# Seven-product blocks of a feed-forward: earlier loads, one sum moved from a DMA to GpSimd, stream sums moved forward

## The chip, the cores and the metric

The kernel runs on one core of a Trainium2 chip. The metric is the device time of one execution in microseconds (us). The engines are named as the profile names them: PE is TensorE's matmul, PEld its weight load, DVE is VectorE, ACT is ScalarE, POOL is GpSimd, SP is SyncE, which here only issues DMAs.

## What is computed

The reference is a two-layer trunk over 256 latent tokens and 256 context tokens of width 1024. Each layer does a SwiGLU feed-forward half-step, a mixer with three head groups, and a second feed-forward half-step; both streams use the same weights. The change touches one of the four feed-forwards, the first of layer 1:

```python
def swiglu(h, w1, w2):
    g, u = jnp.split(h @ w1, 2, axis=-1)
    return (jax.nn.silu(g) * u) @ w2
x   = x   + 0.5 * gate_x * swiglu(ada_rms(x,   ...), w1, w2)
ctx = ctx + 0.5 * gate_c * swiglu(ada_rms(ctx, ...), w1, w2)
```

Width 2816 is handled as 22 column blocks of 128, in two halves of 11 (`JH`).

## The kernel before, in words

Every operand is held as a high part (float32r) and a low part (the rest), so that a product is three matmuls: high by high, high by low, low by high. ACT makes the high part of a weight tile (a cast), DVE the low part (a subtraction of two SBUF tiles). The tokens lie along the free dimension: columns 0 to 255 are the latent stream, 256 to 511 the context.

In three of the feed-forwards a column block is computed directly: gate and up weights by both streams at once. In layer 1's first feed-forward the first four blocks of the first half are direct (`DIRECT = 4`); the first two of these take the latent stream's products first and the context's after them, since the context's norm is later. The other 7 blocks of the first half and all 11 of the second are seven-product blocks (class `Seven`): the 2x2 block product of (gate, up halves) by (latent, context) is done with seven products of half size instead of eight. This needs sums of weights and sums of the streams:

- `sums` (line 463) makes four sums of the two streams in two rounds `q` of 12 steps, on DVE, with ACT casting each result to `th` and DVE writing the rest to `tl`. The steps are put in the list `bg` ahead of the direct blocks 2 and 3 (line 671); `pump`, called after each product, takes one step for each 512 columns of product.
- `load(j)` (line 493) lets SP load the gate block into a `wr` buffer (three of these) and the up block's first half twice into `cb[:, j % 2]`, and POOL add two more halves to it by DMAs with an accumulating write (lines 502 and 503). This gives `q`.
- `load_u(j)` loads the up block's second half into `ur` (one buffer).
- `second(j)` (line 530) adds `q`'s first half to the first half of `wr`, by an accumulating DMA from POOL. It overwrites what `low("g", j)` reads. `fourth(j)` (line 534, L537) adds the two halves of `wr` on DVE. The result is `r`.
- `high` and `low` make the parts of `g`, `q`, `r` and `u`. The parts `wh` and `wl` have four buffers each.

`go` (line 559) issues a block's seven products of 12 matmuls each on PE, in the order g, q, g, q, r, r, u, and the combinations of their results on DVE and ACT (L583 to L593). After each product it calls `nxt(slot)`, which places the preparation of the next block between: `high("g")` at slot 0, `low("g")` and `second` at 1, `high("q")` and `load_u` at 2, `low("q")` and the load of the block after next at 3, `fourth` and `high("r")` at 5, `low("r")` at 6, where the high part of the gated result (`aTh`) has just been made. Each engine and each DMA queue works its instructions in the order in which they are issued here, and waits by semaphores alone. The first seven-product block of a half is prepared by the list `prepare(j)`: in the last direct block for the first half, beside the last `down` products for the second.

Of the kernel before, what the change touches and what calls it, by code (L numbers as in the profile page):

```python
# [20 lines left out]
KT = D // 128  # L21
# [111 lines left out]
def tile_hybrid_dit(ctx: ExitStack, tc: tile.TileContext, t_x, t_c, t_cb, t_ada0, t_ada, t_adab, t_nw, t_w1, t_w2,  # L133
# [42 lines left out]
    def flush_due():  # L176
        while due:
            due.pop(0)[1]()
# [38 lines left out]
    with tc.manual_schedule():  # L217
# [230 lines left out]
        class Seven:  # L448
# [14 lines left out]
            def sums(self, q):  # L463
# [13 lines left out]

                def parts(i, n, sign=1.0):
                    h, lo = self.th[:, i, k0], self.tl[:, i, k0]
                    S.activation(out=h, in_=x[n], func=AF.Copy, scale=sign)  # L480
                    V.scalar_tensor_tensor(out=lo, in0=x[n], scalar=sign, in1=h.bitcast(F32), op0=ALU.mult,
                                           op1=ALU.subtract)

                def comb(n, p, r, op):
                    V.tensor_tensor(out=x[n], in0=x[p], in1=x[r], op=op)

                return [lambda: (work(), whole(0, k0, b)), lambda: whole(1, k0, a),
                        lambda: comb(1, 1, 0, ALU.subtract), lambda: parts(0, 1),
                        lambda: whole(2, k1, b), lambda: comb(0, 2, 0, ALU.subtract), lambda: parts(2, 0),
                        lambda: comb(2, 2, 1, ALU.add), lambda: parts(1, 2, -1.0),  # L490
                        lambda: whole(0, k1, a), lambda: comb(0, 2, 0, ALU.subtract), lambda: parts(3, 0)]

            def load(self, j):
                if j >= 2 * JH:
                    return
                g, u = t_w1[self.l, self.f, j, 0], t_w1[self.l, self.f, j, 1]
                r = wpool.tile([128, CHUNK], F32, tag="wr", name="wr", bufs=RAW_BUFS)
                SP.dma_start(out=r, in_=g)
                q = cb[:, j % 2]
                for k in range(2):  # L500
                    SP.dma_start(out=q[:, 512 * k:512 * k + 512], in_=u[:, 0:512])
                G.dma_start(out=q[:, 0:512], in_=u[:, 512:1024], accum_op=ALU.add)
                G.dma_start(out=q[:, 512:1024], in_=g[:, 0:512], accum_op=ALU.add)
                self.raw["g", j] = self.raw["r", j] = r
                self.raw["q", j] = q

# [23 lines left out]
            def second(self, j):  # L530

                G.dma_start(out=self.raw["r", j][:, 0:512], in_=self.raw["q", j][:, 0:512], accum_op=ALU.add)

# [5 lines left out]
            def prepare(self, j):  # L539

                return [lambda: self.high("g", j), lambda: (self.low("g", j), self.second(j)),
                        lambda: self.high("q", j), lambda: self.low("q", j), lambda: self.fourth(j),
                        lambda: self.high("r", j), lambda: self.low("r", j)]

# [54 lines left out]
        def ffn(l, f, lead, norms, steps=None, tail=None):  # L599
# [7 lines left out]
            with tc.tile_pool(name="ffn", bufs=1) as fp:  # L607
# [5 lines left out]
                for half in range(2):  # L613
# [34 lines left out]
                    if half == 0 and not one:  # L648
# [5 lines left out]
                        for c, kt in LEAD[lead]:  # L654
                            if c == len(w):
                                w.append(ws.take(0))
                            up(w[c], ps[c], a, b, kt)
                        flush_due()
                        for j in range(2):
                            for a, b in first[1:]:  # L660
# [6 lines left out]
                    if seven and half == 0:  # L667
                        first_j = seven.prepare(j1)
                        seven.load(j1)
                        seven.load(j1 + 1)  # L670
                        bg.extend([s for q in range(2) for s in seven.sums(q)] + [lambda: seven.load_u(j1)])
                        pace[0], pace[1] = SUMS, 0.0
                    for j in range(j0, j1):
# [13 lines left out]
                    for j in range(j1, JH if seven else j1):  # L687
                        n = half * JH + j

                        def nxt(slot):  # L690
# [12 lines left out]
                            elif slot == 0:  # L703
                                seven.high("g", n + 1)
                            elif slot == 1:
                                seven.low("g", n + 1)
                                seven.second(n + 1)
                            elif slot == 2:
                                seven.high("q", n + 1)
                            elif slot == 3:  # L710
                                seven.low("q", n + 1)
                                if j < JH - 2:
                                    seven.load(n + 2)
                            elif slot == 5:
                                seven.fourth(n + 1)
                                seven.high("r", n + 1)
                            elif slot == 6:
                                seven.low("r", n + 1)

# [9 lines left out]
                    for m in range(KT - 2 if split_tail else KT):  # L729
                        a, b = 0, T * len(streams)  # L730
                        wa, wb = ws.take(), ws.take(AHEAD - 1)
                        ps = mm_bank("d")
                        if seven and half == 0:
                            if m == KT - 3:
                                seven.load(JH)
                                seven.load(JH + 1)
                            if m >= KT - 2:
                                for s in seven.prepare(JH)[0 if m == KT - 2 else 4:4 if m == KT - 2 else 8]:
                                    s()
                        down(m, wa, wb, a, b, ps)  # L740
                        residual(l, i, m, ps, 0, streams)
                        if half == 1:
# [1036 lines left out]
```

## Time and profile before

| | |
|---|---|
| time, median of 3 runs | 1876.81 us (1873.68 to 1882.07) |
| the profiled execution | 1881.24 us, its span 1879.5 us |
| PE busy | 1815.5 us, 97% of the span |
| PEld, DVE, ACT, POOL busy | 82%, 65%, 37%, 9% |
| mean DMA traffic | 150 GB/s |

The span is the time from the first to the last instruction; the execution's own time has 1.7 us more around it. A busy share is an average over stages with different limits, so the rows below are taken from the stage that the change touches, 1060 to 1420 us. The granted clock (PEclk) is 1.00 at TensorE's level of 2.4 GHz and 0.50 at 1.2 GHz.

### The profile page before, as it was taken

The page shows a single profiled execution, that of the slowest core. Times are in us where ns is not written, and L with a number is a line of the kernel's source. Part 1 is how long each engine was busy: PE and PEld are TensorE (multiplying, and loading weights), DVE is VectorE, ACT ScalarE, POOL GpSimd, SP SyncE. Part 2 cuts the span into 40 slices and gives each one's busy share as a digit, 9 for nine tenths or more (in the row PEclk, how much of TensorE's full clock was granted, in tenths as well). Part 3 has the DMA queues.
Part 4 walks back from the last instruction along what each step waited for, and adds up shares of the span by engine and source line. Part 5 has one row for each costly group of instructions (what it writes and reads, how often), then busy time and mean ns, then how long its engine had stood idle before and what let it go on. Part 6 is the DMA issues. An engine that isn't in the chain of part 4 may idle for free. (4 is left out here: it accounts for less than half of the span.)

```text
span 1879.5 us, 27717 instructions
## 1 busy us (share of the span) xinstructions
PE 1815.5 (97%) x10944; PEld 1542.7 (82%) x10944; DVE 1213.8 (65%) x2064; ACT 690.9 (37%) x1131; POOL 174.9 (9%) x207
## 2 busy tenths in 40 slices
PE   7999999999999999999999988898889999999999
PEld 5788888887669888888888878888887877889999
DVE  5788778665455658777777576735664645666665
ACT  3332222245542333222222334423433455354443
POOL 0000000002133300000000001101210113410000
PEclk9999999999999999999999999999999999999999
DMA  7755656333121226555576335645763342335655
GB/s 292 261 177 193 201 181 200 113 110 118 56 63 45 68 68 222 182 171 199 184 264 230 97 99 136 163 121 122 176 162 101 100 130 68 112 117 169 191 176 157
DMA packets 96835, 281.72 MB, mean 150 GB/s; under 512 B 11329, under 2 KB 18113, under 8 KB 96577
## 3 DMA queue, kind: packets, MB, share of 16 engines
q1 hardware_dynamic: 88928, 265.79, 43.2%
q0 software_dynamic: 7776, 14.16, 4.8%
q8 instruction: 86, 1.41, 0.3%
q14 instruction: 45, 0.36, 0.1%
HBM read 274.14 MB, written 1.05 MB: 146 GB/s over the span
## 5 line engine op out<-in xcount | busy, mean ns | idle before, releaser
L98 DVE TENSOR_TENSOR wl<-wr,wh 128x1024 fp32r<-128x1024 f32 (+1 forms) x340 | 364.3, 1100 | 107.2 <-ACT wh L87 105.8
L87 ACT CAST wh<-wr 128x1024 fp32r<-128x1024 f32 (+1 forms) x340 | 312.2, 945 | 187.9 <-PE d L205 124.6
L204 PE MATMUL d<-aTh,wh 128*128 128x512 f32 (+1 forms) x770 | 268.9, 349 | 0.0
L205 PE MATMUL d<-aTl,wh 128*128 128x512 f32 (+1 forms) x770 | 268.4, 349 | 0.0
L206 PE MATMUL d<-aTh,wl 128*128 128x512 f32 (+1 forms) x770 | 268.4, 349 | 0.0
L204 PE MATMUL g<-hTh,wh 128*128 128x512 f32 (+2 forms) x592 | 208.6, 352 | 1.5 <-ACT wh L87 0.5
L205 PE MATMUL g<-hTl,wh 128*128 128x512 f32 (+2 forms) x592 | 208.3, 352 | 1.3 <-DVE hTl L354 1.1
L206 PE MATMUL g<-hTh,wl 128*128 128x512 f32 (+2 forms) x592 | 207.5, 351 | 0.6 <-DVE wl L98 0.5
L206 PE MATMUL u<-hTh,wl 128*128 128x512 f32 (+2 forms) x592 | 207.4, 350 | 0.4 <-DVE wl L98 0.4
L204 PE MATMUL u<-hTh,wh 128*128 128x512 f32 (+2 forms) x592 | 207.0, 350 | 0.0
L205 PE MATMUL u<-hTl,wh 128*128 128x512 f32 (+2 forms) x592 | 206.9, 350 | 0.0
L204 PEld LDWEIGHTS d<-aTh,wh 128*128 128x128 f32 x770 | 144.5, 188 | 21.3
L205 PEld LDWEIGHTS d<-aTl,wh 128*128 128x128 f32 x770 | 144.5, 188 | 21.2
L206 PEld LDWEIGHTS d<-aTh,wl 128*128 128x128 f32 x770 | 144.5, 188 | 21.2
L278 DVE CUSTOM_DVE_ANT_0 aw<-aw,cb 128x1024 f32<-128x1024 f32 x128 | 155.0, 1223 | 2.4
L212 PE MATMUL nat<-wh,hTh 128*128 128x512 f32 (+2 forms) x384 | 137.1, 357 | 0.0
L637 ACT CAST aTh<-sg 128x512 fp32r<-128x512 f32 x66 | 40.9, 619 | 256.0 <-DVE sg L633 242.3
L429 DVE SCALAR_TENSOR_TENSOR xT<-d,mod,xT 128x256 f32<-128x256 f32 x112 | 50.3, 480 | 126.6 <-PE d L206 126.6
L214 PE MATMUL nat<-wh,hTl 128*128 128x512 f32 (+2 forms) x384 | 128.0, 333 | 0.4 <-DVE hTl L354 0.4
L213 PE MATMUL nat<-wl,hTh 128*128 128x512 f32 (+2 forms) x384 | 127.7, 333 | 0.0
L204 PEld LDWEIGHTS g<-hTh,wh 128*128 128x128 f32 x592 | 111.6, 189 | 19.0 <-ACT hTh L371 1.5
L205 PEld LDWEIGHTS g<-hTl,wh 128*128 128x128 f32 x592 | 111.9, 189 | 17.9 <-DVE hTl L354 2.3
(261 smaller groups left out, 3432.2 us busy)
## 6 DMA issues: line engine op xcount, KB each, us to landing
wr<-in_w_dram SPq DMA_DIRECT2D x158, 512.0 KB, 4.3
aw<-in_ada_dram SPq DMA_DIRECT2D x144, 512.0 KB, 5.4
wr<-in_wi_dram SPq DMA_DIRECT2D x56, 512.0 KB, 3.6
wr<-in_w_dram SPq DMA_DIRECT2D x64, 384.0 KB, 3.7
wr<-in_w_dram SPq DMA_DIRECT2D x64, 320.0 KB, 2.9
cb<-in_w_dram SPq DMA_DIRECT2D x36, 256.0 KB, 5.8
cb<-in_w_dram POOLq DMA_DIRECT2D x36, 256.0 KB, 4.5
wr<-in_wo_dram SPq DMA_DIRECT2D x16, 512.0 KB, 3.6
```

The source lines that it names most:

```text
L87: self.nc.scalar.copy(out=h[:, :n], in_=self.raw[i][:, :n])
L98: self.nc.vector.tensor_tensor(out=lo[:, :n], in0=t[:, :n], in1=h[:, :n].bitcast(F32), op=ALU.subtract)
L204: PE.matmul(out=ps, lhsT=wh[:, col:col + 128], rhs=hh[rhs_sl], start=start, stop=False)
L205: PE.matmul(out=ps, lhsT=wh[:, col:col + 128], rhs=hl[rhs_sl], start=False, stop=False)
L206: PE.matmul(out=ps, lhsT=wl[:, col:col + 128], rhs=hh[rhs_sl], start=False, stop=stop)
L212: PE.matmul(out=ps, lhsT=hh[lhs_sl], rhs=wh[:, wc], start=start, stop=False)
L213: PE.matmul(out=ps, lhsT=hh[lhs_sl], rhs=wl[:, wc], start=False, stop=False)
L214: PE.matmul(out=ps, lhsT=hl[lhs_sl], rhs=wh[:, wc], start=False, stop=stop)
L278: V.tensor_tensor_reduce(out=junk, in0=t, in1=cb[:, s], scale=1.0, scalar=0.0, op0=ALU.mult, op1=ALU.add, accum_out=mod[l][:, 8 * r + b, s ...
L429: V.scalar_tensor_tensor(out=xT[:, m, s * T:s * T + T], in0=ps[:, s * T - c0:s * T - c0 + T], scalar=mod[l][:, 24 * i + 16 + m, s:s + 1], ...
L637: S.copy(out=aTh[:, j], in_=sg)
```

## The change

- `sums` issues the same work in another order: a cast follows directly on its sum, and the subtraction behind it stands one sum later. Its first step asks that the norms of both streams have been issued.
- These steps, and `load_u(DIRECT)`, go in the list ahead of the context's products of the first two direct blocks, at the same pace of one step for 512 columns. The adding DMAs of the first two seven-product blocks follow in the list.
- `load` is split: SP's loads stay in `load`, POOL's two adding DMAs are `add`. In a block, `load` of the block after next moves from slot 3 to slot 0 and `add` to slot 4.
- `second` is an addition on POOL instead of an accumulating DMA.
- `high("g")` moves from slot 0 of a block to slot 6 of the block before it, `low("g")` and `second` from slot 1 to slot 0. `prepare` ends with the `high("g")` of the block after it.
- In the last `down` products of the first half the preparation is issued behind the products of its `m` instead of in front of them.

```diff
--- before.py
+++ after.py
@@ -475,20 +475,27 @@
                 def whole(n, k, c):
                     V.tensor_tensor(out=x[n], in0=hTh[:, k, c].bitcast(F32), in1=hTl[:, k, c].bitcast(F32), op=ALU.add)
 
-                def parts(i, n, sign=1.0):
-                    h, lo = self.th[:, i, k0], self.tl[:, i, k0]
-                    S.activation(out=h, in_=x[n], func=AF.Copy, scale=sign)
-                    V.scalar_tensor_tensor(out=lo, in0=x[n], scalar=sign, in1=h.bitcast(F32), op0=ALU.mult,
-                                           op1=ALU.subtract)
+                def high(i, n, sign=1.0):
+                    S.activation(out=self.th[:, i, k0], in_=x[n], func=AF.Copy, scale=sign)
+
+                def low(i, n, sign=1.0):
+                    V.scalar_tensor_tensor(out=self.tl[:, i, k0], in0=x[n], scalar=sign,
+                                           in1=self.th[:, i, k0].bitcast(F32), op0=ALU.mult, op1=ALU.subtract)
 
                 def comb(n, p, r, op):
                     V.tensor_tensor(out=x[n], in0=x[p], in1=x[r], op=op)
 
-                return [lambda: (work(), whole(0, k0, b)), lambda: whole(1, k0, a),
-                        lambda: comb(1, 1, 0, ALU.subtract), lambda: parts(0, 1),
-                        lambda: whole(2, k1, b), lambda: comb(0, 2, 0, ALU.subtract), lambda: parts(2, 0),
-                        lambda: comb(2, 2, 1, ALU.add), lambda: parts(1, 2, -1.0),
-                        lambda: whole(0, k1, a), lambda: comb(0, 2, 0, ALU.subtract), lambda: parts(3, 0)]
+                def normed(f):
+                    f.when = lambda: all(kt in feeds[self.l, 2 * self.f, n].done for kt in range(KT) for n in range(2))
+                    return f
+
+                sub = ALU.subtract
+                return [normed(lambda: (work(), whole(0, k0, b))), lambda: whole(1, k0, a),
+                        lambda: (comb(1, 1, 0, sub), high(0, 1)), lambda: whole(2, k1, b),
+                        lambda: low(0, 1), lambda: (comb(0, 2, 0, sub), high(2, 0)),
+                        lambda: (comb(2, 2, 1, ALU.add), high(1, 2, -1.0)), lambda: low(2, 0),
+                        lambda: whole(0, k1, a), lambda: low(1, 2, -1.0),
+                        lambda: (comb(0, 2, 0, sub), high(3, 0)), lambda: low(3, 0)]
 
             def load(self, j):
                 if j >= 2 * JH:
@@ -499,10 +506,16 @@
                 q = cb[:, j % 2]
                 for k in range(2):
                     SP.dma_start(out=q[:, 512 * k:512 * k + 512], in_=u[:, 0:512])
+                self.raw["g", j] = self.raw["r", j] = r
+                self.raw["q", j] = q
+
+            def add(self, j):
+
+                if j >= 2 * JH:
+                    return
+                g, u, q = t_w1[self.l, self.f, j, 0], t_w1[self.l, self.f, j, 1], self.raw["q", j]
                 G.dma_start(out=q[:, 0:512], in_=u[:, 512:1024], accum_op=ALU.add)
                 G.dma_start(out=q[:, 512:1024], in_=g[:, 0:512], accum_op=ALU.add)
-                self.raw["g", j] = self.raw["r", j] = r
-                self.raw["q", j] = q
 
             def load_u(self, j):
                 if j >= 2 * JH:
@@ -529,7 +542,8 @@
 
             def second(self, j):
 
-                G.dma_start(out=self.raw["r", j][:, 0:512], in_=self.raw["q", j][:, 0:512], accum_op=ALU.add)
+                r = self.raw["r", j]
+                G.tensor_tensor(out=r[:, 0:512], in0=r[:, 0:512], in1=self.raw["q", j][:, 0:512], op=ALU.add)
 
             def fourth(self, j):
 
@@ -539,8 +553,9 @@
             def prepare(self, j):
 
                 return [lambda: self.high("g", j), lambda: (self.low("g", j), self.second(j)),
-                        lambda: self.high("q", j), lambda: self.low("q", j), lambda: self.fourth(j),
-                        lambda: self.high("r", j), lambda: self.low("r", j)]
+                        lambda: self.high("q", j), lambda: self.low("q", j),
+                        lambda: (self.fourth(j), self.high("r", j)), lambda: self.high("g", j + 1),
+                        lambda: self.low("r", j)]
 
             def product(self, ps, w, j, k, t):
                 wh, wl = self.part[w, j]
@@ -656,6 +671,10 @@
                                 w.append(ws.take(0))
                             up(w[c], ps[c], a, b, kt)
                         flush_due()
+                        if seven:
+                            bg.extend([s for q in range(2) for s in seven.sums(q)])
+                            bg.append(lambda: seven.load_u(DIRECT))
+                            pace[0], pace[1] = SUMS, 0.0
                         for j in range(2):
                             for a, b in first[1:]:
                                 for kt in range(KT):
@@ -665,11 +684,10 @@
                             ws.prefetch(j + 2)
                     j1 = DIRECT * (1 - half) if seven else JH
                     if seven and half == 0:
-                        first_j = seven.prepare(j1)
                         seven.load(j1)
                         seven.load(j1 + 1)
-                        bg.extend([s for q in range(2) for s in seven.sums(q)] + [lambda: seven.load_u(j1)])
-                        pace[0], pace[1] = SUMS, 0.0
+                        bg.extend([lambda: seven.add(j1), lambda: seven.add(j1 + 1)])
+                        first_j = seven.prepare(j1)
                     for j in range(j0, j1):
                         if seven and j == j1 - 1:
                             bg.extend(first_j)
@@ -701,20 +719,22 @@
                                 elif slot in (1, 3, 5):
                                     ws.prefetch((slot + 1) // 2)
                             elif slot == 0:
-                                seven.high("g", n + 1)
-                            elif slot == 1:
                                 seven.low("g", n + 1)
                                 seven.second(n + 1)
+                                if j < JH - 2:
+                                    seven.load(n + 2)
                             elif slot == 2:
                                 seven.high("q", n + 1)
                             elif slot == 3:
                                 seven.low("q", n + 1)
-                                if j < JH - 2:
-                                    seven.load(n + 2)
+                            elif slot == 4 and j < JH - 2:
+                                seven.add(n + 2)
                             elif slot == 5:
                                 seven.fourth(n + 1)
                                 seven.high("r", n + 1)
                             elif slot == 6:
+                                if j < JH - 2:
+                                    seven.high("g", n + 2)
                                 seven.low("r", n + 1)
 
                         seven.go(n, lambda sg, between: gated(j, sg, between), nxt)
@@ -730,14 +750,15 @@
                         a, b = 0, T * len(streams)
                         wa, wb = ws.take(), ws.take(AHEAD - 1)
                         ps = mm_bank("d")
-                        if seven and half == 0:
-                            if m == KT - 3:
-                                seven.load(JH)
-                                seven.load(JH + 1)
-                            if m >= KT - 2:
-                                for s in seven.prepare(JH)[0 if m == KT - 2 else 4:4 if m == KT - 2 else 8]:
-                                    s()
+                        if seven and half == 0 and m == KT - 3:
+                            seven.load(JH)
+                            seven.load(JH + 1)
+                            seven.add(JH)
+                            seven.add(JH + 1)
                         down(m, wa, wb, a, b, ps)
+                        if seven and half == 0 and m >= KT - 2:
+                            for s in seven.prepare(JH)[slice(0, 4) if m == KT - 2 else slice(4, 7)]:
+                                s()
                         residual(l, i, m, ps, 0, streams)
                         if half == 1:
                             for s in streams:
```

## Rows read from the trace of the kernel before

**Rows 1.** Windows: length, busy time (instructions) of each engine, granted clock, DMA share
```profile
1122.35:1129.08 6.73, 0.16 (x1) 0.00 (x0) 4.37 (x8) 2.87 (x5) 0.00 (x0) 0.81 0.07 22
1129.08:1215.12 86.04, 75.15 (x589) 72.13 (x589) 59.11 (x77) 36.40 (x57) 14.93 (x17) 0.98 0.62 150
...
1276.72:1417.84 141.12, 119.94 (x925) 115.31 (x924) 91.53 (x121) 56.05 (x87) 24.68 (x28) 0.96 0.67 154
1391.42:1401.35 9.93, 9.93 (x87) 9.93 (x86) 7.09 (x10) 4.14 (x7) 2.52 (x3) 1.00 0.69 164
```

**Rows 2.** Waits from 1129 to 1418 us: who waited for whom, total, times, longest
```profile
DVE wl L527 <- ACT wh L518: 47.1, 32, 4.5
ACT wh L518 <- DMA cb<-in_w_dram: 43.7, 14, 4.8
...
PE p L556 <- DVE wl L527: 27.0, 25, 1.7
...
DVE wr L537 <- DMA wr<-cb: 20.7, 10, 6.7
```

**Rows 3.** Timeline of DVE, one block: start, duration, [idle time before and its releaser]
```profile
1383.88 0.69 DVE L593 SCALAR_TENSOR_TENSOR sg<-cu,sg 128x512 f32<-128x512 f32 x1 [0.88 <-ACT cu L592]
1384.48 1.22 DVE L527 TENSOR_TENSOR wl<-wr,wh 128x1024 fp32r<-128x1024 f32 x1
...
1386.47 1.23 DVE L527 TENSOR_TENSOR wl<-wr,wh 128x1024 fp32r<-128x1024 f32 x1 [0.17 <-ACT wh L518]
1387.61 0.68 DVE L527 TENSOR_TENSOR ul<-ur,uh 128x512 fp32r<-128x512 f32 x1
1390.11 1.23 DVE L527 TENSOR_TENSOR wl<-cb,wh 128x1024 fp32r<-128x1024 f32 x1 [1.81 <-ACT wh L518]
1391.25 0.68 DVE L583 TENSOR_TENSOR sg<-p,a 128x512 f32<-128x512 f32 x1
...
1393.04 0.69 DVE L537 TENSOR_TENSOR wr<-wr 128x512 f32<-128x512 f32 x1
...
1395.20 0.69 DVE L593 SCALAR_TENSOR_TENSOR sg<-cu,sg 128x512 f32<-128x512 f32 x1 [0.87 <-ACT cu L592]
```

**Rows 4.** Timeline of ACT in the same block
```profile
1384.60 0.62 ACT L637 CAST aTh<-sg 128x512 fp32r<-128x512 f32 x1 [0.76 <-DVE sg L593]
...
1385.39 1.05 ACT L518 CAST wh<-wr 128x1024 fp32r<-128x1024 f32 x1
1386.34 0.62 ACT L518 CAST uh<-ur 128x512 fp32r<-128x512 f32 x1
```

**Rows 5.** The second adding DMA, line L503, all 18
```profile
DMA to landing us min/median/max: 4.3/5.6/8.0
```

**Rows 6.** DMA queues from 1276.72 to 1417.84 us: packets, MB, share of 16 engines
```profile
q0 software_dynamic: 4298, 7.82, 35.3%
```

**Rows 7.** Timeline of DVE in the mixer, beside POOL's additions
```profile
583.81 0.68 DVE L799 TENSOR_TENSOR cen<-cen,r 128x512 f32<-128x512 f32 x1
586.02 1.75 DVE L799 TENSOR_TENSOR cen<-cen,r 128x512 f32<-128x512 f32 x1 [1.53 <-POOL r L796]
```

**Rows 8.** Timeline of POOL in the mixer
```profile
585.96 1.27 POOL L1232 TENSOR_TENSOR cen<-cen,gates 128x512 f32<-128x512 f32 x1
...
612.62 2.25 POOL L1232 TENSOR_TENSOR cen<-cen,gates 128x512 f32<-128x512 f32 x1
```

**Rows 9.** Timeline of DVE from the context's norm to the first stream sums
```profile
1092.45 0.48 DVE L354 SCALAR_TENSOR_TENSOR hTl<-t,mod,hTh 128x256 fp32r<-128x256 f32 x1 [0.18 <-ACT hTh L371]
1094.86 0.69 DVE L633 TENSOR_TENSOR sg<-sg,u 128x512 f32<-128x512 f32 x1 [1.92 <-ACT sg L632]
...
1097.18 2.36 DVE L98 TENSOR_TENSOR wl<-wr,wh 128x1024 fp32r<-128x1024 f32 x2 [0.26 <-ACT wh L87]
...
1105.16 1.29 DVE L476 TENSOR_TENSOR sum<-hTh,hTl 128x512 f32<-128x512 f32 x2
```

**Rows 10.** Timeline of PE: the third direct block's first matmul
```profile
1100.08 0.39 PE L204 MATMUL g<-hTh,wh 128*128 128x512 f32 x1
```

## The prediction

> **What bounds the kernel now.** I read the page's busy shares and slices first: TensorE (PE) is busy in nearly every slice, so time can only come from where PE waits, and the slices name such places inside layer 1's first feed-forward, where the change is. Then windows over that stage. The 7 seven-product blocks of the first half last 86.04 us and the 11 of the second 141.12 us [rows 1]: 227.16 us, or 12.62 us a block. One block, the second half's tenth (1391.42 to 1401.35), ran without a wait in 9.93 us [rows 1]; that is PE's own length for one. So 227.16 - 18 x 9.93 = 48.4 us of the stage are waiting, and time at the clock's lower level that followed it (granted clock 0.98 and 0.96 instead of 1.00). In front of the first block PE stands for 6.73 us with 0.16 us of work [rows 1].
>
> Then the waits: PE waits for VectorE (DVE) writing low weight parts, 27.0 us; DVE waits for ScalarE's (ACT) high parts, 47.1 us; ACT waits for the DMAs into `cb`, 43.7 us; and DVE's weight sum at L537 waits 20.7 us for the DMA from `cb` to `wr` [rows 2]. Read backwards this is one loop: the sum `q` in `cb` lands late, DVE is late, its late reads hold up SP's next loads (L511, in front of L498 in SP's queue, waits for DVE's `low("u")`), and the next `q` is late again.
>
> Last, DVE's own cycle, from one L593 to the next, 1383.88 to 1395.20 [rows 3]: 11.32 us. Two waits on ACT stand in it, 1.81 us for `q` and 0.17 for `g`. Without a wait a follower starts about 0.08 us before the end in front of it, so they cost 1.89 + 0.25 = 2.1 us. DVE alone needs 9.2 us a block, PE 9.93: with the waits gone PE is the bound, by 0.7 us.
>
> **The change, part by part.**
>
> *Loads at slot 0, adds at slot 4.* SP runs ahead of PE and only its semaphores hold it. Today the load of block n+2 stands behind `load_u(n+1)`, which waits for `low("u", n)`; now it stands in front of that and needs only `q(n)`'s readers, done a block earlier. I cost the move of SP's three loads at nothing, hidden under a whole block. The two adding DMAs now stand on GpSimd (POOL) behind `second(n+1)` instead of in front of the next one. With T = 0 at L593, `low("g")` ends at 0.60 + 1.14 + 0.60 + 1.22 = 3.6, the POOL sum at 5.3 (below), and the second add is issued 0.7 later, at 6.0. It lands 5.6 us after issue in the median and 8.0 at most [rows 5]: 11.6. ACT asks for it in the next cycle, after the copy to `aTh`, `high("g")`, the copy of the first product and `high("u")`: 1386.34 + 0.62 - 1383.88 = 3.1 after that L593 [rows 3, 4], so at 10.3 + 3.1 = 13.4. 1.8 us are in hand, and 43.7 us of waits go.
>
> *`high("g")` one slot earlier.* Same instruction, now ahead of the copy of the first product on ACT. `low("g")`'s 0.25 us goes. ACT then ends `high("q")` at 3.1 + 1.05 = 4.15, and DVE comes to `low("q")` at 4.1: even.
>
> *The sum on POOL.* A DMA and its landing (DVE's 20.7 us) go, and a POOL addition of two 128x512 SBUF tiles comes. Nearest row: L1232, same shape, also in place, 1.27 us [rows 8]. Alone it is hidden: `low("g")` ends at 3.6, `fourth` starts at 4.1 + 1.14 + 1.79 = 7.0. There is a price [rows 7, 8]. DVE's L799 takes 0.68 us by itself and 1.75 when it starts 0.06 us behind that POOL addition: it stood still until POOL had ended. The other way round, L1232 takes 2.25 instead of 1.27 when it comes behind a DVE subtraction. After `low("g")` DVE runs `low("u")` (to 4.16) and `low("q")`, both with two SBUF inputs. No row shows who is next where both wait. Lower end: DVE keeps going, POOL adds from 5.3 to 6.6, still ahead of `fourth`: 0. Upper end: POOL goes in between and `low("q")` pays the whole 1.27. I take 1.1 (POOL, already waiting, works about 1.1 us from 4.16, and `low("q")` ends at 6.4 instead of 5.3), because each waiter there was served after one instruction. DVE's cycle becomes 9.2 + 1.1 = 10.3, over PE's 9.93 by 0.35. DVE can be late for a while: `low("r")` ends 0.60 + 1.22 = 1.8 us after L593, and L593 starts some 1.8 us after PE ends a block, so 3.6 us into the next one, and PE needs it after 50 of that block's 84 matmuls, at 5.9. 2.2 us of room absorb six blocks. In the second half, which starts with idle DVE, 5 of 11 blocks pay; in the first half, with DVE full just before, all 7: 12 x 0.35 = 4.2 us.
>
> The Trainium skill (SBUF — State Buffer, "Who interferes with whom") says that a DVE instruction with two SBUF inputs and a GpSimd instruction that reads SBUF exclude each other for the whole instruction, whichever issues first. The trace agrees on that [rows 7, 8]. By the page a block would pay the full 1.27, 0.54 over PE: room for four blocks, 14 that pay, 7.6 instead of 4.2 us.
>
> *Streams' sums among the context's first products.* 24 DVE instructions of about 0.65 us (1.29 for two [rows 9]) move forward by some 12 us and take the ACT casts with them; what DVE does is the same. Sixteen of the 24 fall among the context's 32 products (a step for two products). DVE is free of the norm at 1092.93; eight of them, 5.2 us and some 0.9 us of dependence, put the first gate's L633 at 1099.0 instead of 1094.86, and the two splits behind it at 1101.3 instead of 1097.18 [rows 9]. PE begins the third direct block at 1100.08 [rows 10]; its cast is then ready at 1101.3 and its first split at 1102.5, for its third matmul: +2.1 us. From there to the first seven-product block DVE has 24 sums (15.6), three gates (2.8 each with their waits), four splits (4.7) and one `low("g")` (1.2), 29.9 us from 1092.9, so 1122.8, and the direct blocks end at 1122.35 + 2.1. With 1.6 us in hand the 6.6 us stand goes; an overrun would come back one for one.
>
> *The rest*: the `when` on the first step holds already when the steps are queued, and moving `prepare(JH)` behind `down` passes only PE instructions; `second` there no longer waits behind the adds' landings. Nothing for either.
>
> **Sum.** Profiled run 1881.24 (span 1879.5 and 1.7 around it): -6.6 + 2.1 - 48.4 + 4.2 = -48.7, so 1832.5. The median shown, 1876.81, lies 4.4 below the profiled run: **1828**.
>
> **Rivals.**
> 1. *The lock costs nothing* (lower end above): 4.2 less, 1824. For: `low("q")` may be dispatched while `low("u")` still runs, as in most pairs of [rows 3]. Against: POOL has waited 0.3 us by then.
> 2. *The adds collide with loads pulled ahead.* The adds of block n+2 now share the DMA engines with loads of n+3. Two blocks form a loop: `low("q")` to L593 5.1, L593 to POOL's end 5.3, 0.7 to the second issue, landing, 1.15 for cast and start: 12.25 + landing. It binds over 10.3 a block from a landing of 8.3 us; 8.0 was the longest [rows 5]. The engines were busy 0.67 of the second half [rows 1], some 8.6 us a block, which in 10.3 us is 0.84 before the removed DMA (one in three of the adding queue's, itself 35.3% [rows 6]) is taken off, about 0.7 after. If some 4 us of a block's loads are put on each median landing, 9.6: 10.9 a block, 18 x 0.97 less the 4.2 above, +13 us: 1841.
> 3. *The adds land as late as ever*: a landing of 13 us gives 12.6 a block, the block gains nothing, and only the stand goes: 1876.8 - 4.5 = 1872. For: the adds still come last on POOL. Against: the room above.
> 4. *Slower*: the same loop with landings of 15.5 us, POOL's addition and the next loads in front of each pair of adds: 13.9 a block, 18 x 3.97 = 71.5 us over PE's own length where it is 48.4 now, so 1876.8 - 4.5 + 23 = 1895. It decides from about 13.5 us. For: POOL is one queue in order. Against: nearly twice the longest landing, with fewer bytes to move.
>
> **How the numbers follow.** Forecast 0.50 (own range 1822 to 1835), lock free 0.13, collision 0.22 (reaching to 1855), no gain 0.07, slower 0.08. The range 1820 to 1856 holds the first three, 0.85. A measurement of this kernel tells about 0.5%, 9.4 us, from no change: faster 0.85, same 0.07, slower 0.08.
>
> **What would show it.** Blocks of 10.0 to 10.4 us; no wait of ACT on the `cb` DMA; a POOL addition of 1.3 to 1.9 us a block, with the DVE instruction beside it 1.1 longer; PE's 6.6 us before the first block gone, and some 2 us at the third direct block. Wrong if blocks stay above 11.5 us, if DVE's `low` parts stand at 1.2 while PE still waits, or if PE waits more than 5 us among the direct blocks.

## The result and the profile after

The changed kernel took 1830.06 us, the median of four runs (1828.06 to 1833.68), beside 1875.24 us for the kernel before on the same chip: a ratio of 0.9756 with the interval [0.9724, 0.9788], so 2.4% faster. Its profiled execution took 1833.68 us, with a span of 1831.9.

The whole difference is in the stage of the change. From one matmul that both kernels run in the first direct block (L206, at 1075.51 us before and 1076.12 after) to the end of the last seven-product block the one before took 342.33 us and the changed one 294.17, 48.2 less; the rest of the program took 1537.1 and 1537.8. Windows of the changed kernel, in the columns of [rows 1]: the last 2.78 us in front of the first block, the first half's 7 blocks, the second half's 11, one block of these.

```profile
1122.20:1124.98 2.78, 2.78 (x13) 2.25 (x12) 2.29 (x3) 2.10 (x3) 0.64 (x2) 1.00 0.91 231
1124.98:1197.80 72.82, 71.39 (x590) 69.95 (x588) 61.74 (x76) 35.23 (x56) 20.27 (x17) 1.00 0.58 147
1259.39:1370.29 110.90, 110.46 (x925) 109.51 (x924) 95.54 (x117) 53.95 (x85) 31.49 (x28) 1.00 0.62 158
1289.17:1299.10 9.93, 9.93 (x87) 9.93 (x85) 7.28 (x10) 4.83 (x8) 3.34 (x3) 1.00 0.83 222
```

The halves fell from 86.04 and 141.12 us to 72.82 and 110.90. At PE's own 9.93 us a block they would be 69.5 and 109.2, so 5.0 us of waiting are left of 48.4. The granted clock is 1.00 throughout, where it was 0.98 and 0.96. The last two direct matmuls of the first half and the first of the new block stand next to each other:

```profile
1124.75 0.40 PE L206 MATMUL u<-hTh,wl 128*128 128x512 f32 x1
1124.98 0.28 PE L569 MATMUL p<-hTh,wh 128*128 128x256 f32 x1
```

Here PE stood for 6.73 us before. The waits of the changed kernel from 1124 to 1371 us, as [rows 2] (total, times, longest):

```profile
DVE wl L540 <- ACT wh L531: 13.0, 10, 2.6
...
ACT wh L531 <- DMA cb<-in_w_dram: 6.8, 5, 2.6
...
DVE wr L551 <- POOL wr L546: 2.5, 2, 1.3
...
PE p L571 <- DVE wl L540: 1.1, 3, 0.6
```

The loop is gone: PE's wait for the low parts from 27.0 to 1.1 us, DVE's for the casts from 47.1 to 13.0, ACT's for `cb` from 43.7 to 6.8, the weight sum's from 20.7 (for a DMA) to 2.5 (for POOL). DVE's own cycle, as [rows 3]:

```profile
1160.68 0.69 DVE L608 SCALAR_TENSOR_TENSOR sg<-cu,sg 128x512 f32<-128x512 f32 x1 [0.89 <-ACT cu L607]
1161.30 1.22 DVE L540 TENSOR_TENSOR wl<-wr,wh 128x1024 fp32r<-128x1024 f32 x1
1162.43 0.69 DVE L655 TENSOR_TENSOR aTl<-sg,aTh 128x512 fp32r<-128x512 f32 x1
1163.03 1.22 DVE L540 TENSOR_TENSOR wl<-wr,wh 128x1024 fp32r<-128x1024 f32 x1
1164.17 0.69 DVE L540 TENSOR_TENSOR ul<-ur,uh 128x512 fp32r<-128x512 f32 x1
1164.77 2.32 DVE L540 TENSOR_TENSOR wl<-cb,wh 128x1024 fp32r<-128x1024 f32 x1
1167.01 0.68 DVE L598 TENSOR_TENSOR sg<-p,a 128x512 f32<-128x512 f32 x1
...
1168.79 0.68 DVE L551 TENSOR_TENSOR wr<-wr 128x512 f32<-128x512 f32 x1
...
1170.96 0.69 DVE L608 SCALAR_TENSOR_TENSOR sg<-cu,sg 128x512 f32<-128x512 f32 x1 [0.88 <-ACT cu L607]
```

From one L608 (L593 in the kernel before) to the next 10.28 us (11.32 before), with no wait on `q` or `g`. The fourth L540, `low("q")`, is the one to look at: it follows `low("u")` without idle time and yet takes 2.32 us, where its equals take 1.22. POOL in the same block:

```profile
1164.39 1.61 POOL L546 TENSOR_TENSOR wr<-wr,cb 128x512 f32<-128x512 f32 x1 [6.94 <-DVE wl L540]
1165.96 0.87 POOL L517 DMA_DIRECT2D cb<-in_w_dram  x1
1166.56 1.18 POOL L518 DMA_DIRECT2D cb<-in_w_dram  x1
```

The POOL sum is issued at 1164.39, while `low("u")` runs, and ends at 1166.00; `low("q")`, taken up at 1164.77, ends 1.09 us after that, nearly a whole length of its own. So POOL went first and DVE stood. This is what is called the lock below: of two engines one stands until the other's instruction has ended.

### The profile page after: what moved, and what is told of

Its sections match the earlier page's. It is cut to its first block, busy times and chain, and to the rows that moved or that the text cites. A ratio compares the mean times of both kernels' runs of the same rounds, so it can differ in the third digit from the quotient of the medians.

```text
span 1831.9 us, 27737 instructions
## 1 busy us (share of the span) xinstructions
PE 1802.7 (98%) x10944; PEld 1534.8 (84%) x10944; DVE 1225.2 (67%) x2064; ACT 690.0 (38%) x1131; POOL 188.0 (10%) x207
## 5 line engine op out<-in xcount | busy, mean ns | idle before, releaser
L206 PE MATMUL d<-aTh,wl 128*128 128x512 f32 (+1 forms) x770 | 268.4, 349 | 0.0
L206 PE MATMUL g<-hTh,wl 128*128 128x512 f32 (+2 forms) x592 | 207.6, 351 | 1.1 <-DVE wl L98 1.1
L206 PE MATMUL u<-hTh,wl 128*128 128x512 f32 (+2 forms) x592 | 207.4, 350 | 0.4 <-DVE wl L98 0.4
L206 PEld LDWEIGHTS d<-aTh,wl 128*128 128x128 f32 x770 | 144.5, 188 | 21.2
```

The source lines that it names most:

```text
L206: PE.matmul(out=ps, lhsT=wl[:, col:col + 128], rhs=hh[rhs_sl], start=False, stop=stop)
```

## The experiments

Ratios are against the kernel before, run beside each on the same chip. "Stage" is the two halves' windows; PE alone needs 69.5 and 109.2 us.

| kernel | median us | ratio, interval | first half | second half |
|---|---|---|---|---|
| before | 1875 to 1877 | 1 | 86.04 | 141.12 |
| the change | 1830.06 | 0.9756 [0.9724, 0.9788] | 72.82 | 110.90 |
| s1: sums alone | 1870.69 | 0.9964 [0.9948, 0.998] | 86.15 | 139.15 |
| s4: loads alone | 1855.01 | 0.9882 [0.9867, 0.9897] | 80.34 | 121.16 |
| p1: POOL sum alone | 1850.9 | 0.986 [0.9833, 0.9887] | 78.69 | 119.78 |
| s2: all but the POOL sum | 1845.06 | 0.9829 [0.9814, 0.9844] | 79.77 | 117.91 |
| p2: all but the early cast | 1834.58 | 0.9769 [0.9737, 0.98] | 74.19 | 112.27 |
| p3: a second POOL operation | 1832.44 | 0.9762 [0.9733, 0.9792] | 74.28 | 110.18 |
| s3: the sum on DVE | 1826.85 | 0.9733 [0.9716, 0.975] | 70.37 | 109.18 |
| p4: sum on DVE, sums later | 1828.49 | 0.9738 [0.9712, 0.9764] | 69.48 | 109.20 |
| c1: the change, 5 rounds | 1829.11 | 0.9752 [0.9737, 0.9768] | 72.78 | 110.58 |
| c2: s3, 5 rounds | 1827.2 | 0.9738 [0.9723, 0.9753] | 70.36 | 109.19 |
| c3: s3, sums at half pace | 1827.33 | 0.974 [0.9725, 0.9755] | 71.88 | 109.19 |

**One part alone, or all but one.** s1 is the kernel before with `sums` in the new order and in the new place, nothing else:

```diff
                         flush_due()
+                        if seven:
+                            bg.extend([s for q in range(2) for s in seven.sums(q)])
+                            bg.append(lambda: seven.load_u(DIRECT))
+                            pace[0], pace[1] = SUMS, 0.0
```

> The kernel before with the streams' sums in the new order and place, nothing else changed. Theory A (the parts of the prediction): PE's stand of 6.6 us in front of the first seven-product block goes, the third direct block starts 2 us late, the blocks stay at 12.6 us on average; with the stretch of lower clock behind the stand gone too, 5 to 7 us less than before: 1869 us. Rival B (VectorE is only filled elsewhere, and the first block waits as long): 1875 us.

It gained 6.8 us, in the range. In its trace, from the matmul named above to the first block, it takes 48.87 us where the kernel before takes 53.58: 4.7 less, the stand gone and the third direct block later, as the prediction's -6.6 and +2.1 have it. The first half is as long as before (86.15 us) and the second 2.0 shorter (139.15), which was not followed up. So the stand was DVE's sums, and nearly all of the blocks' waits had nothing to do with them.

s4 is the kernel before with the loads ahead and the adds apart:

```diff
                             elif slot == 0:
                                 seven.high("g", n + 1)
+                                if j < JH - 2:
+                                    seven.load(n + 2)
...
                                 seven.low("q", n + 1)
-                                if j < JH - 2:
-                                    seven.load(n + 2)
+                            elif slot == 4 and j < JH - 2:
+                                seven.add(n + 2)
```

> The kernel before with the loads of a block at slot 0 and the adding DMAs apart from them at slot 4, nothing else changed (the weight sum by DMA, the cast of g at slot 0, the sums beside the direct blocks 2 and 3). Theory A: ScalarE's wait for the sum in cb goes, VectorE's wait for the DMA into wr stays: cycle 9.45 + 2 = 11.5 us, PE's stand in front of the first block stays: 1853 to 1860 us. Rival C (the place of the loads hardly matters): 1870 to 1876 us.

1855.01, as expected, with blocks of 11.0 to 11.3 us where 11.5 had been worked out. ACT's wait for `cb` fell from 43.7 us to one of 4.5; what was left is in the waits of s4 from 1127 to 1391 us:

```profile
DVE wr L543 <- DMA wr<-cb: 33.0, 18, 5.0
...
ACT wh L524 <- DMA cb<-in_w_dram: 4.5, 1, 4.5
```

The weight sum by DMA is now late in all 18 blocks, where it was late in 10. p1 is the other half of it, the kernel before with the sum on POOL and the loads where they were:

```diff
-                G.dma_start(out=self.raw["r", j][:, 0:512], in_=self.raw["q", j][:, 0:512], accum_op=ALU.add)
+                r = self.raw["r", j]
+                G.tensor_tensor(out=r[:, 0:512], in0=r[:, 0:512], in1=self.raw["q", j][:, 0:512], op=ALU.add)
```

> The kernel before with the sum of second() on GpSimd, nothing else changed (loads and adding DMAs together at slot 3, the sums beside the direct blocks 2 and 3). Theory A: the sum in cb still lands late, so ScalarE and VectorE wait for it as before; VectorE's wait for the DMA into wr (20.7 us in all) goes, and GpSimd's addition falls where VectorE waits for the cast of q, so it shuts nothing out: blocks of 11.5 to 12 us, 1855 to 1866 us. Rival C (the sum on GpSimd makes most of the gain): blocks under 11 us, 1840 to 1848 us.

1850.9, better than expected by 4 to 15 us, and between the theory's range and rival C's: the blocks last 11.24 us on average in the first half and 10.89 in the second. The waits of p1 from 1128 to 1389 us:

```profile
DVE wl L527 <- ACT wh L518: 32.9, 34, 3.7
...
ACT wh L518 <- DMA cb<-in_w_dram: 29.7, 15, 4.0
```

The expectation kept ACT's 43.7 us for `cb`; they fell to 29.7 without a load having been moved, which fits a loop of which the DMA wait that went was a link. Whether it was this or the adding queue, which has one DMA in three less, no run tells apart. s2, the changed kernel with the sum by DMA again, says the same from the other side:

```diff
-                G.tensor_tensor(out=r[:, 0:512], in0=r[:, 0:512], in1=self.raw["q", j][:, 0:512], op=ALU.add)
+                G.dma_start(out=self.raw["r", j][:, 0:512], in_=self.raw["q", j][:, 0:512], accum_op=ALU.add)
```

> The changed kernel with the sum of second() as an accumulating DMA again. Theory A: the sum in cb still lands early, so ScalarE waits little for it, but the DMA into wr lands 5 us after its issue and VectorE's fourth() waits some 2.3 us for it in each block; no instruction is held up by GpSimd. VectorE's cycle 9.2 + 2.3 = 11.5 us, blocks of 11.5 us: 1851 us (1845 to 1858). Rival C (taking one of three accumulating DMAs out of the queue made the gain, the places of loads and adds hardly matter): blocks near 12.5 us, 1866 to 1870 us.

1845.06, some 6 us under the expected 1851, at the edge of the range: `fourth` waits 35.5 us for the DMA, 2.0 a block, since that DMA lands 4.8 us after issue in the median. Alone the POOL sum brought 25.2 us and the loads 22.5, the sums 6.8: 54.5, with the early cast still to come, where all together brought 45.2 (47.7 in c1). In the blocks alone, by the traces, it is clearer: 28.7, 25.7 and 1.9, together some 56, against 43.4. On top of the others the POOL sum brought 1845 - 1830 = 15. These parts do not add up, as parts that cut the same loop would not.

p2 leaves out only the early cast, with the step by which `low("g")` and `second` had followed it to slot 0:

```diff
                             elif slot == 0:
-                                seven.low("g", n + 1)
-                                seven.second(n + 1)
+                                seven.high("g", n + 1)
                                 if j < JH - 2:
                                     seven.load(n + 2)
+                            elif slot == 1:
+                                seven.low("g", n + 1)
+                                seven.second(n + 1)
...
-                                if j < JH - 2:
-                                    seven.high("g", n + 2)
```

> The changed kernel with the cast of g at slot 0 of its own block's turn again, low part of g and GpSimd's sum at slot 1. Theory A: VectorE waits 0.25 us a block for that cast again, cycle 10.27 + 0.25 = 10.5 us, 14 of 18 blocks pay: 3 to 4 us more than the changed kernel, 1834 us. Rival E (the place of this cast is worth nothing, VectorE has the time): 1830 us. Rival F (the cast a block ahead is what breaks the chain): 1845 us or more.

1834.58, the expected time: blocks in which DVE sets the pace last some 10.53 us, not 10.27. But 11 of the 18 pay, not 14, and the two halves are 2.7 us longer than the change's, under the 3 to 4 expected. By the times alone rival E is not excluded, since the intervals of p2 and the change overlap; the trace speaks against it. The place, in p2's DVE timeline:

```profile
1184.48 1.23 DVE L540 TENSOR_TENSOR wl<-wr,wh 128x1024 fp32r<-128x1024 f32 x1 [0.17 <-ACT wh L531]
```

This is the 0.17 of [rows 3] again; with the 0.08 by which a follower starts early it is the 0.25 predicted, and the blocks show 0.26.

**The lock.** My theory was that the 0.35 us a block over PE come from POOL's sum holding up `low("q")`; the rival, that they come from POOL's queue (adds issued later) or from the adds' landing. s3 takes the changed kernel's sum to DVE:

```diff
-                G.tensor_tensor(out=r[:, 0:512], in0=r[:, 0:512], in1=self.raw["q", j][:, 0:512], op=ALU.add)
+                V.tensor_tensor(out=r[:, 0:512], in0=r[:, 0:512], in1=self.raw["q", j][:, 0:512], op=ALU.add)
```

> The changed kernel with the sum of second() as an addition on VectorE instead of GpSimd. Theory A (GpSimd's addition costs VectorE 1.1 us a block because it shuts out an instruction with two SBUF inputs; the addition on VectorE itself costs 0.6): VectorE's cycle 9.2 + 0.6 = 9.8 us, under PE's 9.93, low parts all at 1.22 us, blocks of 9.93 us in the second half and at most 10.1 in the first: 5 us less than the changed kernel, 1825 us. Rival D (the long subtraction beside GpSimd is not lost time, VectorE has no more room): blocks of 10.3 us or more, 1830 to 1840 us.

1826.85, and every block but two lasts 9.93 us. DVE of s3 in one block:

```profile
1307.40 1.22 DVE L540 TENSOR_TENSOR wl<-wr,wh 128x1024 fp32r<-128x1024 f32 x1
1308.65 0.69 DVE L546 TENSOR_TENSOR wr<-wr,cb 128x512 f32<-128x512 f32 x1
1309.26 0.69 DVE L540 TENSOR_TENSOR ul<-ur,uh 128x512 fp32r<-128x512 f32 x1
1309.86 1.22 DVE L540 TENSOR_TENSOR wl<-cb,wh 128x1024 fp32r<-128x1024 f32 x1
```

DVE does one instruction more, for 0.6 us of its time, and `low("q")` is back at 1.22: an addition given to POOL had cost DVE 1.1 us, one of its own costs 0.6. p3 asks whether any POOL work costs DVE that much; it puts a second POOL operation, a product with ones, behind the sum:

```diff
+                e = r[:, 0:512].rearrange("p (a b) -> p a b", a=8)
+                G.tensor_tensor(out=e, in0=e, in1=ones.unsqueeze(1).to_broadcast([128, 8, HD]), op=ALU.mult)
```

> The changed kernel with a second GpSimd instruction behind the sum, a multiplication by one of the same 512 columns in place, so that results are the same. Theory A (GpSimd and VectorE exclude each other only while VectorE's instruction has two SBUF inputs): it waits for VectorE's low part of q and then runs beside the three instructions that read PSUM; VectorE's cycle stays at 10.3 us, the adding DMAs land 2 us later and still in time: 1830 to 1832 us. Rival G (whatever GpSimd does at that time VectorE loses): 1.1 to 1.3 us a block more, blocks of 11.4 us, 1848 to 1852 us.

1832.44. POOL's busy time in the two halves rose from 51.8 to some 89 us and the second half did not grow (110.18). POOL's product in one block of p3:

```profile
1326.50 2.16 POOL L548 TENSOR_TENSOR wr<-wr,ones 128x512 f32<-128x512 f32 x1
```

DVE beside it:

```profile
1325.74 1.76 DVE L540 TENSOR_TENSOR wl<-cb,wh 128x1024 fp32r<-128x1024 f32 x1 [0.46 <-ACT wh L531]
1327.43 0.68 DVE L600 TENSOR_TENSOR sg<-p,a 128x512 f32<-128x512 f32 x1
1328.14 0.69 DVE L602 TENSOR_TENSOR cu<-p,sg 128x512 f32<-128x512 f32 x1
```

The two instructions that read `p`, which lies in PSUM (the memory that PE writes its results to), keep their 0.68 and 0.69 us, as in all 18 blocks. POOL's product takes 1.30 us where nothing holds it up (the shortest of its 18), so some 0.9 of the 2.16 us was standing until `low("q")` had ended at 1327.50, and only the rest ran beside them. It reads no `cb`, so a tile that both read is not what makes them stand. The first half grew by 1.5 us, but by another road: in its first block, where the preparation has no block to hide under, `fourth` stood 2.56 us behind POOL (1.18 in the changed kernel). After it DVE's cycle is 10.27 us as before. So the queue is no cause either: the adds go out 2.2 us later, ACT waits for `cb` in 13 blocks instead of 5 (12.4 us), and the running blocks don't pay for it.

**The collision.** Where the landing of the second adding DMA went is read from six kernels (least, median and longest, us):

| | loads moved ahead | second add lands after |
|---|---|---|
| before, [rows 5] | no | 4.3 / 5.6 / 8.0 |
| p1 | no | 4.2 / 5.3 / 7.2 |
| s4 | yes | 5.0 / 7.7 / 8.6 |
| the change | yes | 5.6 / 7.4 / 9.1 |
| p3, adds 2.2 us later | yes | 5.0 / 5.8 / 7.7 |
| s3, adds some 3 us earlier | yes | 4.8 / 6.7 / 8.4 |

With the loads pulled ahead it is 1 to 2 us longer, but with adds issued 2.2 us later nearly as before. The times of issue fit a collision: in one block of the change SP's two loads into `cb` are issued at 1298.43 and 1298.85, behind the adds (1296.52 and 1297.11), and the second add lands at 1304.77, amid them; in p3 they go out ahead of the adds, at 1296.47 and 1296.89, and have landed by 1300.03. That the overlap is the cause was not tested by itself.

**The third direct block.** In the changed kernel PE waits there:

```profile
1101.77 0.50 PE L204 MATMUL g<-hTh,wh 128*128 128x512 f32 x1 [0.93 <-ACT wh L87]
1102.11 0.40 PE L205 MATMUL g<-hTl,wh 128*128 128x512 f32 x1
1103.03 0.50 PE L206 MATMUL g<-hTh,wl 128*128 128x512 f32 x1 [0.53 <-DVE wl L98]
```

p4 (s3 with the streams' sums begun behind the first gate, at twice the pace) was to take this wait away:

```diff
-                        if seven:
-                            bg.extend([s for q in range(2) for s in seven.sums(q)])
...
                             ws.prefetch(j + 2)
+                            if seven and j == 0:
+                                bg.extend([s for q in range(2) for s in seven.sums(q)])
+                                bg.append(lambda: seven.load_u(DIRECT))
+                                pace[0], pace[1] = 2 * SUMS, 0.0
```

> The changed kernel with the sum of second() on VectorE, and the streams' sums started behind the first gate and its two splits instead of in front of them, at two steps for 512 columns while the context's products last. Theory A: blocks of 9.93 us as with the sum on VectorE alone, and the 1.8 us that PE waited at the third direct block go; VectorE is as full in front of the first seven-product block as before: 1825 us, 2 us less than with the sum on VectorE alone. Rival B: the sums end later and the first seven-product block waits for them, 1828 to 1830 us.

It came out at 1828.49, the rival's time, though not at the rival's place: the wait came back one block later, at the fourth direct block, and behind it a stretch at a lower granted clock, 0.83 on average (0.50, the lower level, from 1112 to 1118 us). PE of p4 there:

```profile
1111.97 0.80 PE L204 MATMUL g<-hTh,wh 128*128 128x512 f32 x1 [2.38 <-ACT wh L87]
```

The window around it, up to the first seven-product block, in the columns of [rows 1]:

```profile
1106.81:1126.41 19.60, 17.19 (x61) 12.99 (x60) 16.04 (x22) 8.67 (x13) 1.76 (x2) 0.83 0.53 135
```

All 18 blocks then last 9.93 us, but the way to the first of them is 3.9 us longer than in s3.

c1, c2 and c3 measured the change, s3, and s3 with half the pace during the context's products and 1.3 times of it after, in five rounds:

```diff
-                            pace[0], pace[1] = SUMS, 0.0
+                            pace[0], pace[1] = 0.5 * SUMS, 0.0
...
                         first_j = seven.prepare(j1)
+                        pace[0] = 1.3 * SUMS
```

> The changed kernel once more, as the measure for the two beside it: 0.9756 of the kernel before, some 1830 us, blocks of 9.93 us for the first six of the second half and 10.3 us otherwise.

> The changed kernel with the sum of second() on VectorE, again, beside the changed kernel on the same chip. Theory A: 18 blocks of 9.93 us, 4 to 5 us less than the changed kernel. Rival D (the two are the same within what can be measured): less than 2 us apart.

> As c2, and the streams' sums at half the pace beside the context's first products (four of them in front of the first gate instead of eight), then at 1.3 steps for 512 columns. Theory A (the third direct block waits because its splits stand behind the sums in VectorE's queue): each sum less in front of the first gate is 0.65 us, so PE's 1.8 us there go and the blocks stay at 9.93: 1.5 to 2 us less than c2, as the trace shows it; the median can hardly tell. Rival B: the wait comes back at the fourth direct block or in front of the first seven-product block, as it did with the sums behind the gate: c2 or more.

c1 repeats the change, 1829.11. c2 is at 1827.2: 1.9 us by the medians and 3.8 us in the traces' stage, where 4 to 5 had been expected. Their intervals against the kernel before overlap, but each of c2's four runs (1825.91 to 1827.80) is shorter than any of c1's five (1827.86 to 1831.18), so the sum on DVE is the faster one, by some 2 us. c3 is at 1827.33: the wait at the third direct block went and returned in the first seven-product block. PE of c3 there:

```profile
1123.26 0.39 PE L569 MATMUL p<-hTh,wh 128*128 128x256 f32 x1 [0.31 <-ACT wh L531]
...
1124.52 0.39 PE L571 MATMUL p<-hTh,wl 128*128 128x256 f32 x1 [0.76 <-DVE wl L540]
```

From the matmul named above to the end of the last block c2 takes 289.98 us, c3 289.96 and p4 292.96: halving the pace moved the wait and gained nothing, starting later cost 3.0 us in the trace, which the medians cannot tell. In the changed kernel DVE needs 31.1 us from the context's norm to the end of the first block's `low("g")`, 5.5 of it waits for ACT, and PE begins the block 0.4 us after that. In this stretch DVE is full, and where the sums stand chooses which matmul waits.

## Why the prediction was right

The predicted time was 1828 us, worked out as 1832.5 for the profiled execution; these came out at 1830.06 and 1833.68. By its steps:

- *The stand* of 6.6 us in front of the first block: gone whole (6.73 by the window), as predicted; s1 shows that it goes by the sums alone, with the next term taken off (4.7).
- *The third direct block, +2.1*: 2.0, from the two waits above (0.93 for the cast, 0.53 for the split) and the slower matmuls beside them, by the mechanism given. Of the 1.6 us in hand before the first block only 0.4 was left: DVE took 31.1 us where 29.9 had been added up, and `low("g")` ended at 1124.62, the block beginning at 1124.98. This sum was 1.2 too small, and the margin hid it:

```profile
1123.39 1.23 DVE L540 TENSOR_TENSOR wl<-wr,wh 128x1024 fp32r<-128x1024 f32 x1 [0.26 <-ACT wh L531]
```

- *The waits of the blocks, -48.4*: gone but for the excess below.
- *The lock*: of the two ends, 0 and 1.27 us, the prediction took 1.1. Measured 2.32 - 1.22 = 1.10 where `low("q")` had not to wait for its cast (7 of 10 blocks that the second half prepares for itself), and s3 shows that it is this addition. POOL's sum itself took 1.61 us in the median, within the 1.3 to 1.9 foreseen (1.29 to 2.20 in all). p3 shows that DVE instructions reading PSUM pay nothing. Rival 1, the lock free, fell. The Trainium skill (SBUF — State Buffer, "Who interferes with whom") says that a DVE instruction with two SBUF inputs and a GpSimd one that reads SBUF exclude each other for the whole instruction. The trace agrees on that: `low("q")` got through only after the POOL sum had ended. The full 1.27 that the prediction worked out by it, with 14 blocks that pay and 7.6 us, came out as 1.10, 12 blocks and 5.0.
- *The excess, 12 blocks at 0.35 = 4.2*: all 7 blocks of the first half and 5 of the 11 of the second ran at 10.13 to 10.77 us, six of the second at 9.93, so the count was exact and so was the usual price (10.25 to 10.29). The repeat, c1, has the seventh block of its second half at 9.95, so the exact count has some luck in it. It came to 5.0: the second half 1.7, as predicted (5 x 0.35), the first 3.3 instead of 2.45. This term was a little too small: two blocks of the first half took 10.77 and 10.55. In the first PE waited 0.56 us for the low part of `r`; in the second DVE's wait before L608 was 1.17 us instead of 0.89. Why these two waits came was not tried.
- *The adds*: predicted to land in 5.6 us with 1.8 in hand. The landing was mis-sized: 7.4 in the median, as rival 2 (the collision) had foreseen in kind. But 5.6 + 1.8 = 7.4 just covers it, the loop of two blocks binds only above 8.3 (two of the 18 landings were longer, 8.5 and 9.1), and ACT waited five times, 6.8 us in all, which the prediction had at none. That the margin was just as large as the miss is luck. Where it waited, DVE lost little. In one such block of the changed kernel:

```profile
1145.05 1.49 DVE L540 TENSOR_TENSOR wl<-cb,wh 128x1024 fp32r<-128x1024 f32 x1 [0.75 <-ACT wh L531]
```

0.75 of waiting and 1.49 of work are 2.24 us, no more than the 2.32 without a wait: POOL's addition ran while DVE was waiting anyway, so the wait and the lock overlap. Rivals 3 and 4 needed landings of 13 us and more; the longest was 9.1.

So the mechanism was right, and margins carried it where a size was off: the landing and DVE's work before the first block were both taken too small, and both were hidden. The sum holds to 1.2 us of the profiled execution: the excess was 0.8 too small, the stand and the direct block together came out 0.2 better, and the program outside the stage took 0.6 us more.

## What to carry to other kernels

When several waits close into one loop through queues and buffers, price the loop: take the longest of the engines' own cycles and of the transfers' round trips as the new period; the gains of the edits taken one at a time will not add up. Before moving an elementwise sum to a slower idle engine, look at what the busy engine does in the same microseconds: here the move cost VectorE 1.1 us where doing the sum itself cost 0.6. And where an engine is full from one fixed point to another, moving work inside that stretch moved the wait (c3) or lengthened it (p4); something has to leave it.

## What the runs showed that was not expected

- A DVE instruction that followed another without idle time still had to stand for a POOL addition issued during the one before it (2.32 instead of 1.22 us, in both halves).
- POOL's second operation stood some 0.9 us of its 2.16 for DVE's subtraction and ran the rest beside DVE instructions that read PSUM, which paid nothing, though POOL's busy time rose by some 37 us.
- The same adding DMA took 5.3 to 5.6 us to land, 6.7 to 7.7 with loads of the next block pulled ahead, and 5.8 when issued 2.2 us later.
- The kernel with the sum on DVE (s3, c2) is faster than the change: by 3.8 us in the traces' stage, and by 1.9 us in the medians of c2 and c1, 1827.2 and 1829.11, with no run of c2 as long as any of c1.
